# Softmax times V for 96 heads: products of two heads packed densely into one accumulator, with zeros beside each head's probabilities

## The chip, the core and the metric

The kernel runs on one NeuronCore of a Trainium2 chip. The metric is the time of one execution on the device in microseconds (us); lower is better. A core has a matrix engine (PE, whose weight loads are listed as PEld), a vector engine (DVE), an activation engine (ACT), a general engine (POOL) and a queue engine (SP) that here only issues DMA transfers. The engines run side by side, each takes its own instructions in order, and they wait for each other by semaphores: counters that an instruction raises when it has finished and that another engine's instruction waits on.

## What is computed

```python
batch, n_heads, seq, head_dim = 8, 12, 1024, 64
scores: [8, 12, 1024, 1024] float32      v: [8, 12, 1024, 64] float32

attn = np.exp(scores - scores_max)
attn = attn / (np.sum(attn, axis=-1, keepdims=True) + 1e-8)
return np.matmul(attn, v)
```

There are 96 heads. The scores are 402.7 MB, V and the output 25.2 MB each. The fast path leaves the maximum out (exp of the raw score), takes the row sums from a column of ones beside V, and checks at the end that all sums and all V lay in a safe range ("the verdict"); if they did not, a slow general path computes everything anew. With the inputs used here the general path is not taken.

## The kernel before, in words

**Tiling.** Two heads form a pair (T = 2). A pair's scores are loaded as one tile s_nat of 128 partitions: partitions 0 to 63 belong to the first head, 64 to 127 to the second, and each partition holds R = 16 whole score rows of 1024 keys (8.4 MB). So "row r" below means 128 score rows, 64 of each head. The loop `For_i` (L423) has 24 iterations; each handles four heads, that is K = 2 pairs, k = 0 and k = 1. There is one s_nat buffer for each k.

**One row** (function heads, L366 on):
- ACT computes exp of two rows at once into p_nat (L377; eight buffers of two rows). In the second half of k = 1 it takes one row at a time ("late" rows).
- PE turns the row: eight transposes of 128x128 into psT (L390), each a weight load and a matmul. After it, psT holds for each chunk c of 128 keys: keys on the partitions, 128 columns, 64 for each head.
- DVE copies two rows (one if late) from psT to pt in SBUF (L402, late L398). psT and pt have two buffers of two rows each.
- PE multiplies (function finish, L152): for each of the eight chunks, pt's 128 columns are the weights and `vones` of both heads the moving data: 64 columns of V of head 0, two columns of ones, 64 columns of V of head 1, together M = 130. All eight accumulate into 130 columns of psO. Head 0's rows against head 1's V, and the reverse, are computed too and never read.
- A row is multiplied LAG = 3 rows after it was turned. After each G = 3 rows, DVE takes the reciprocals of the sums (L132) and multiplies: once for partitions 0 to 63 and once for 64 to 127, since the useful columns differ (L140). This is function normalise; with 16 rows there are six groups for each k.

**Around it.** POOL spreads the loaded V into `vones` as half-precision (spread_v, L248). In the middle of k = 0 DVE takes the largest absolute value of `vones` (watch_v, L259, with two small operations at L269). At the end of every iteration DVE and PE work out the verdict so far (judge: two reductions at L285 and L286, small operations at L289 and L292, a product of one column at L297 on PE, a copy at L301).

**Order of the transfers.** SP issues them in one order written out by hand: in an iteration the next pair for k = 0 (load_first, after the last exp of k = 0), the store of k = 0, then in function last the next pair for k = 1, the store of k = 1 and the next V. A load waits until exp has read the buffer. For the very last pairs the loads are cut into parts: two halves for k = 0 of the last iteration, and 4, 4, 3, 2, 1, 1, 1 rows for k = 1 of the last iteration. The nested `If` arms of last choose between these. The stores of the last pair are issued by end (L185).

**What sets the order on PE.** The helper in_line chains every transpose and product in program order, so PE does: turn row r, multiply row r - 3, turn row r + 1, and so on. Every weight load and every matmul of the built program raises PE's one semaphore by one, and all other engines wait on its value. That holds for the changed program as well: it has 769 weight loads and 769 matmuls in an iteration's body, the old one 513 and 513.

Of the kernel before, what the change touches and what calls it, by code (L numbers as in the profile page):

```python
# [9 lines left out]
FP16 = mybir.dt.float16  # L10
# [16 lines left out]
def kernel(  # L27
# [25 lines left out]
    T = 2  # L53
# [28 lines left out]
    s_bufs = buffers(sb_pool, K, [P, R, SK], FP32, "s_nat")  # L82
    v_sb = sb_pool.tile([P, C // L, S, L, D], FP32, name="v_sb")
    p_bufs = buffers(sb_pool, 8, [P, EB, SK], FP16, "p_nat")
    pt_bufs = buffers(sb_pool, 2, [P, EB, SK], FP16, "pt")
    out_bufs = buffers(sb_pool, K, [P, R, D], FP32, "out_sb")
    small_pool = ctx.enter_context(tc.tile_pool(name="small", bufs=1))
    seen = small_pool.tile([P, 1 + K * R + 1], FP32, name="seen")
# [34 lines left out]
            after(dma, queued[-1])  # L123
        queued.append(dma)

    def invert(k, st, g):

        rows = min(G, R - g * G)
        psO = st["psO"][g][:, 0 : rows * M].rearrange("p (g m) -> p g m", m=M)
        at = 1 + k * R + g * G  # L130
        recip = seen[:, at : at + rows].rearrange("p (g o) -> p g o", o=1)
        nc.vector.reciprocal(out=recip, in_=psO[:, :, D : D + 1])  # L132
        return psO, recip

    def normalise(k, st, g):
        psO, recip = invert(k, st, g)
        rows = min(G, R - g * G)
        for t in range(T):
            part = slice(t * W, (t + 1) * W)
            nc.vector.tensor_tensor(  # L140
                out=out_bufs[k][part, g * G : g * G + rows, :],
                in0=psO[part, :, t * N : t * N + D],
                in1=recip[part].to_broadcast([W, rows, D]),
                op=ALU.mult,
            )

    def finish(u):

        n0, k, r, pt, st = u
        g, i = r // G, r % G  # L150
        for c in range(C):
            product = nc.tensor.matmul(  # L152
                out=st["psO"][g][:, i * M : (i + 1) * M],
                lhsT=pt[:, c * P : (c + 1) * P],
                rhs=vones[:, k, c].rearrange("p t n -> p (t n)")[:, 0:M],
                start=(c == 0),
                stop=(c == C - 1),
            )
            in_line(product)
        if i == G - 1 or r == R - 1:  # L160
            normalise(k, st, g)
        if r == R - 1 and k < K - 1:
            spread_v(k)
            store(n0, k)
# [14 lines left out]

    def end():  # L180

        cut = (GROUPS - 2) * G
# [10 lines left out]
    watches = []  # L193
# [50 lines left out]
    def spread_v(k):  # L244

        for t in range(T):
            for s in range(S):
                spread = nc.gpsimd.tensor_copy(  # L248
                    out=vones[s * Q : (s + 1) * Q, k, :, t, 0:D].rearrange(
                        "i (h l) d -> i h l d", l=L  # L250
                    ),
                    in_=v_sb[(k * T + t) * Q : (k * T + t + 1) * Q, :, s],
                )
                for watch in watches:
                    apart(spread, watch, "products in between")

    def watch_v(behind):

        watch = nc.vector.tensor_reduce(  # L259
            out=most,  # L260
            in_=vones[:, :, :, :, 0:D].rearrange("p k c t d -> p k (c t) d"),
            axis=mybir.AxisListType.XYZ,
            op=ALU.max,
            apply_absolute_value=True,
        )
        after(watch, behind)
        watches.append(watch)
        for bound, op in ((V_MIN, ALU.is_ge), (V_MAX, ALU.is_le)):
            nc.vector.scalar_tensor_tensor(  # L269
                out=fits, in0=most, scalar=bound, in1=fits, op0=op, op1=ALU.mult  # L270
            )
# [6 lines left out]
    most, fits, right = small("most"), small("fits"), small("right", FP16)  # L278
    nc.gpsimd.memset(fits, 1.0)

    def judge(bank):

        n = K * R
        part = small("part")
        nc.vector.tensor_reduce(out=seen[:, 0:1], in_=seen[:, 0 : n + 1], axis=X, op=ALU.min)  # L285
        nc.vector.tensor_reduce(  # L286
            out=seen[:, n + 1 : n + 2], in_=seen[:, 1 : n + 2], axis=X, op=ALU.max
        )
        nc.vector.scalar_tensor_tensor(  # L289
            out=part, in0=seen[:, n + 1 : n + 2], scalar=1.0, in1=fits, op0=ALU.is_le, op1=ALU.mult  # L290
        )
        nc.vector.scalar_tensor_tensor(  # L292
            out=right, in0=seen[:, 0:1], scalar=1.0 / SUM_MAX, in1=part, op0=ALU.is_ge, op1=ALU.mult
        )
        cell = bank[0:1, G * M : G * M + 1]
        in_line(
            nc.tensor.matmul(  # L297
                out=cell, lhsT=right[:], rhs=vones[:, 0, 0, 0, D : D + 1], start=True, stop=True
            )
        )  # L300
        nc.vector.tensor_copy(out=count[:], in_=cell)  # L301

    def general():
# [8 lines left out]
        nc.gpsimd.memset(s_bufs[0][:, 3, 0 : C * (D + 1)], 1.0)  # L312
        half = SK // 2
        with tc.For_i(0, BH * C, 1, iteration_sync="reg_based") as n:
            nc.sync.dma_start(out=row, in_=s_rows[bass.ds(n, 1)].rearrange("o p j -> (o p) j"))
            nc.sync.dma_start(
                out=v1[:, :, 0:D], in_=v_rows[bass.ds(n // C, 1)].rearrange("o p c d -> (o p) c d")
            )
# [24 lines left out]
            nc.sync.dma_start(  # L343
                out=o_rows[bass.ds(n, 1)].rearrange("o p d -> (o p) d"), in_=out_row
            )

    def last(n0):

        before = queued[-1:]
        k = K - 1  # L350
        with tc.If(n0 < BH - AHEAD) as cmp:
            spread_v(k)
            with tc.If(n0 < BH - 2 * AHEAD) as cmp2:
                queued[:] = before
                load(k, (n0 + (AHEAD + T * k)) % BH)
                store(n0, k)
                load_v((n0 + 2 * AHEAD) % BH)
            with cmp2.Else():
                queued[:] = before
                load(k, BH - T, (4, 4, 3))  # L360
                store(n0, k)
                load(k, BH - T, (2, 1, 1, 1), 11)
        with cmp.Else():
            queued[:] = before
            end()

    def heads(n0):

        for k in range(K):
            st = dict(psO=[take(psO_bufs) for g in range(GROUPS)])  # L370
            for r in range(R):
# [23 lines left out]
                    in_line(turned)  # L395
                    other_bank(psT2, r % EB, turned)
                if late:
                    copy = nc.vector.tensor_copy(out=pt, in_=psT)  # L398
                    rewrite(pt2, copy)
                    other_bank(psT2, r % EB, copy)  # L400
                elif r % EB == EB - 1:
                    copy = nc.vector.tensor_copy(out=pt2[:], in_=psT2[:])  # L402
# [12 lines left out]

    assert BH % AHEAD == 0 and BH >= 2 * AHEAD and SK == Q * S * C and K == 2
    load_v(0)
    for k in range(K):
        load(k, T * k, (R // 2, R // 2) if k == 0 else (R,))
    for k in range(K):  # L420
        spread_v(k)
    load_v(AHEAD)
    with tc.For_i(  # L423
        0, BH, AHEAD, iteration_sync="reg_based"
# [41 lines left out]
```

## Time and profile before

| quantity | value |
|---|---|
| time, median of three runs | 1070.16 us (1069.1 to 1070.58) |
| the profiled execution's own time | 1069.46 us |
| its span, first to last instruction | 1067.5 us |
| mean granted PE clock | 0.897 of full |
| bytes moved by DMA | 453.06 MB, mean 424 GB/s, queue busy 98.6% of the span |
| PE busy, with 12312 matmuls | 793.6 us |
| DVE busy | 768.8 us |
| ACT busy | 737.3 us |
| exp of two rows (L377) | 1899 ns each |
| copy of two rows (L402) | 1224 ns each |
| normalise, 64x192 (L140) | 355 ns each, two for a group |
| watch_v's reduction (L259) | 2286 ns each, one in an iteration |

The span is what the profile covers; the execution's time is 1.96 us longer. Busy times are sums over the span; matmuls overlap each other, so PE's busy time is not a measure of how close it is to its limit. The distance between the starts of successive matmuls is: in a row of eight transposes at full clock the trace has starts 55 to 56 ns apart, in products of 130 columns 56 and 59 in turn.

### The profile page before, as it was taken

To read this page: it belongs to the slowest core of one execution; us is meant where nothing else is said; L and a number is where in the kernel's file an instruction comes from. 1 tells how busy PE (TensorE), PEld (TensorE's weight loads), DVE (VectorE), ACT (ScalarE), POOL (GpSimd) and SP (SyncE) were. 2 spreads that over 40 slices of the span, in tenths; PEclk is the share of its full clock that TensorE was granted. 3 is DMA by queue.
4 is the path that set the end of the run, shared out by engine and by line. 5 is a ranking of instruction groups with operands and counts; after the bars stand their busy time and mean duration, and the time that the engine had idled before them with its cause. 6 is when DMAs were issued, how large, how long until landed. Compare 5 with 4: busy or idle time off the path is not lost.

```text
span 1067.5 us, 32791 instructions
## 1 busy us (share of the span) xinstructions
PE 793.6 (74%) x12312; PEld 757.7 (71%) x12312; DVE 768.8 (72%) x1539; ACT 737.3 (69%) x504; POOL 239.2 (22%) x399
## 2 busy tenths in 40 slices
PE   2578768786786777867878668776786777866887
PEld 2578668686686776867768668776686777866877
DVE  1578767696686866867769667785686866867788
ACT  3567568666686576856867668667686586756893
POOL 3031131211311203113121131221311303113121
PEclk9889889898898988989989889898898988989899
DMA  9999999999999999999999999999999999999993
GB/s 393 441 438 413 422 462 413 452 413 431 453 413 452 426 419 449 417 433 446 440 425 449 425 423 452 413 428 456 413 452 413 431 453 413 452 410 434 432 429 151
DMA packets 18580, 453.06 MB, mean 424 GB/s; under 512 B 2064, under 2 KB 2192, under 8 KB 8720
## 3 DMA queue, kind: packets, MB, share of 16 engines
q1 hardware_dynamic: 18576, 452.99, 98.6%
q8 instruction: 4, 0.07, 0.0%
HBM read 637.53 MB, written 25.17 MB: 621 GB/s over the span
## 4 chain that ended last, share of the span: by engine, by line
DMA 58%; ACT 27%; issue 6%; PE 3%; PEld 2%; DVE 2%; ACTq 1%; SPq 0%; PEldq 0%; DVEq 0%
DMA s_nat<-in_scores_dram 58%; ACT p_nat L377 26%; PE psO L152 1%; PEld L390 1%; PE psT L390 1%; DVE pt L402 1%; PEld L152 1%; ACTq L377 1%; DVE most L259 0%; ACT L377 0%; DVE pt L398 0%; SPq L219 0%; ACTq L423 0%; DVE seen L132 0%; DVE out_sb L140 0%
## 5 line engine op out<-in xcount | busy, mean ns | idle before, releaser
L377 ACT ACTIVATE p_nat<-s_nat 128x2048 f16<-128x2048 f32 (+1 forms) x480 | 706.5, 1557 | 118.9 <-PE psO L152 42.5
L390 PE MATMUL psT<-ident,p_nat 128*128 128x128 f16 x6144 | 505.4, 232 | 166.2 <-ACT p_nat L377 166.2
L390 PEld LDWEIGHTS <-p_nat 128*128 128x128 f16 x6144 | 425.1, 118 | 176.0 <-ACT p_nat L377 176.0
L402 DVE COPY pt<-psT 128x2048 f16<-128x2048 f16 x288 | 352.4, 1224 | 261.5 <-PE L390 165.2
L152 PE MATMUL psO<-vones,pt 128*128 128x130 f16 x6144 | 486.6, 223 | 62.9 <-DVE fits L269 40.4
L152 PEld LDWEIGHTS <-pt 128*128 128x128 f16 x6144 | 387.8, 99 | 84.7 <-DVE pt L402 55.6
L248 POOL CAST vones<-v_sb 32x512 f16<-32x512 f32 x392 | 238.5, 608 | 813.4 <-PE psT L390 318.6
L140 DVE TENSOR_TENSOR out_sb<-psO,seen 64x192 f32<-64x192 f32 (+1 forms) x576 | 191.8, 333 | 18.0
L377 ACT ACT_TABLE_LOAD x24 | 30.8, 1283 | 195.4 <-DMA s_nat<-in_scores_dram 178.5
L398 DVE COPY pt<-psT 128x1024 f16<-128x1024 f16 x192 | 123.5, 685 | 2.3
L259 DVE TENSOR_REDUCE most<-vones 128x1 f32<-128x2048 f16 x24 | 54.9, 2286 | 0.7
L132 DVE RECIPROCAL seen<-psO 128x3 f32<-128x3 f32 (+1 forms) x288 | 49.3, 171 | 2.8 <-PE L390 1.4
L297 PE MATMUL psO<-vones,right 128*1 128x1 f16 x24 | 3.9, 164 | 41.0 <-DVE right L292 41.0
L297 PEld LDWEIGHTS <-right 128*1 128x1 f16 x24 | 1.9, 79 | 45.3 <-DVE right L292 45.3
L301 DVE CAST count<-psO 1x1 int32<-1x1 f32 x24 | 3.5, 146 | 6.2 <-PE psO L297 6.2
L269 DVE SCALAR_TENSOR_TENSOR fits<-most,fits 128x1 f32<-128x1 f32 x48 | 7.4, 155 | 0.0
L289 DVE SCALAR_TENSOR_TENSOR part<-seen,fits 128x1 f32<-128x1 f32 x24 | 5.3, 220 | 0.8
L285 DVE TENSOR_REDUCE seen<-seen 128x1 f32<-128x33 f32 x24 | 4.5, 188 | 0.8
L292 DVE SCALAR_TENSOR_TENSOR right<-seen,part 128x1 f16<-128x1 f32 x24 | 3.9, 162 | 0.8
L286 DVE TENSOR_REDUCE seen<-seen 128x1 f32<-128x33 f32 x24 | 4.2, 177 | 0.0
L77 DVE MEMSET vones<- 128x64 f16 x1 | 0.1, 112 | 0.8 <-PEq L450 0.8
L74 DVE CAST ident<-ident 128x128 f16<-128x128 f32 x1 | 0.2, 227 | 0.4 <-POOL ident masks.py:199 0.4
(8 smaller groups left out, 1.1 us busy)
## 6 DMA issues: line engine op xcount, KB each, us to landing
s_nat<-in_scores_dram SPq DMA_DIRECT2D x50, 4096.0 KB, 18.7
v_sb<-in_v_dram SPq DMA_DIRECT2D x24, 1024.0 KB, 22.2
out_dram<-out_sb SPq DMA_DIRECT2D x47, 512.0 KB, 16.8
s_nat<-in_scores_dram SPq DMA_DIRECT2D x2, 2048.0 KB, 22.8
s_nat<-in_scores_dram SPq DMA_DIRECT2D x1, 1536.0 KB, 27.5
s_nat<-in_scores_dram SPq DMA_DIRECT2D x3, 512.0 KB, 20.8
s_nat<-in_scores_dram SPq DMA_DIRECT2D x1, 1024.0 KB
s_nat<-in_scores_dram SPq DMA_DIRECT2D x47, 28.4
```

The source lines that it names most:

```text
L132: nc.vector.reciprocal(out=recip, in_=psO[:, :, D : D + 1])
L140: nc.vector.tensor_tensor(out=out_bufs[k][part, g * G : g * G + rows, :], in0=psO[part, :, t * N : t * N + D], in1=recip[part].to_broadcas ...
L152: product = nc.tensor.matmul(out=st["psO"][g][:, i * M : (i + 1) * M], lhsT=pt[:, c * P : (c + 1) * P], rhs=vones[:, k, c].rearrange("p t ...
L248: spread = nc.gpsimd.tensor_copy(out=vones[s * Q : (s + 1) * Q, k, :, t, 0:D].rearrange("i (h l) d -> i h l d", l=L), in_=v_sb[(k * T + t) ...
L259: watch = nc.vector.tensor_reduce(out=most, in_=vones[:, :, :, :, 0:D].rearrange("p k c t d -> p k (c t) d"), axis=mybir.AxisListType.XYZ, ...
L269: nc.vector.scalar_tensor_tensor(out=fits, in0=most, scalar=bound, in1=fits, op0=op, op1=ALU.mult)
L289: nc.vector.scalar_tensor_tensor(out=part, in0=seen[:, n + 1 : n + 2], scalar=1.0, in1=fits, op0=ALU.is_le, op1=ALU.mult)
L297: nc.tensor.matmul(out=cell, lhsT=right[:], rhs=vones[:, 0, 0, 0, D : D + 1], start=True, stop=True)
L377: exp = nc.scalar.activation(out=p_nat[:, g : g + rows, :].rearrange("p r (x v) -> p x r v", v=Q * L), in_=s_bufs[k][:, r + g : r + g + ro ...
L390: turned = nc.tensor.transpose(out=psT[:, c * P : (c + 1) * P], in_=p_row[:, c // L, c % L, :], identity=ident16[:],)
L398: copy = nc.vector.tensor_copy(out=pt, in_=psT)
L402: copy = nc.vector.tensor_copy(out=pt2[:], in_=psT2[:])
```

## The change

1. **Products.** `pt` gets a second copy slot for each chunk: shape [128, 2 rows, C = 8, T = 2, T = 2, W = 64]. For each chunk there are now two blocks of 128 columns. Block 0 holds head 0's 64 columns and 64 zeros, block 1 holds 64 zeros and head 1's columns. The zeros are set once, ahead of the loop; the copies write only slots 0 and 3 of the four (apart_columns). finish issues two products for each chunk, one for each block, each with the 65 columns of its own head (M = 65: V and one column of ones). All sixteen accumulate into the same 65 columns of psO, so partitions 0 to 63 get head 0 and 64 to 127 head 1.
2. **Normalise.** G is 4 and the output of both heads lies in the same columns: one reciprocal and one multiplication over 128 partitions for four rows; four groups for each k.
3. **Watch and verdict.** watch_v reads v_sb (the loaded V in single precision) and no longer `vones`. It stands once ahead of the loop and then in function last, at the end of an iteration, behind the second spread_v, in the arm that all but the last iteration take. The two reductions of judge become fold and stay at the end of every iteration; the rest of judge moves to the arm of the last iteration only, behind the last stores.
4. **Transfers.** In the third iteration from the end, the next pair for k = 1 is loaded in two halves (a third nested `If`). The general path issues its transfers from ACT's queue.
5. **Last rows.** For the last two rows of k = 1 the lag is 2 and no longer 3.

```diff
-    G = 3
+    G = 4
-    M = T * N - 2
-    GROUPS = -(-R // G)
+    M = D + 1
+    GROUPS = R // G
-    pt_bufs = buffers(sb_pool, 2, [P, EB, SK], FP16, "pt")
+    pt_bufs = buffers(sb_pool, 2, [P, EB, C, T, T, W], FP16, "pt")
+    for buf in pt_bufs:
+        nc.vector.memset(buf[:], 0.0)
...
-        for t in range(T):
-            part = slice(t * W, (t + 1) * W)
-            nc.vector.tensor_tensor(
-                out=out_bufs[k][part, g * G : g * G + rows, :],
-                in0=psO[part, :, t * N : t * N + D],
-                in1=recip[part].to_broadcast([W, rows, D]),
-                op=ALU.mult,
-            )
+        nc.vector.tensor_tensor(
+            out=out_bufs[k][:, g * G : (g + 1) * G, :],
+            in0=psO[:, :, 0:D],
+            in1=recip.to_broadcast([P, G, D]),
+            op=ALU.mult,
+        )
+    def apart_columns(at):
+        return at[:, :, 0 : 2 * T : 2 * T - 1, :]
...
         for c in range(C):
-            product = nc.tensor.matmul(
-                out=st["psO"][g][:, i * M : (i + 1) * M],
-                lhsT=pt[:, c * P : (c + 1) * P],
-                rhs=vones[:, k, c].rearrange("p t n -> p (t n)")[:, 0:M],
-                start=(c == 0),
-                stop=(c == C - 1),
-            )
-            in_line(product)
+            for t in range(T):
+                product = nc.tensor.matmul(
+                    out=st["psO"][g][:, i * M : (i + 1) * M],
+                    lhsT=pt[:, c, t].rearrange("p u j -> p (u j)"),
+                    rhs=vones[:, k, c, t, 0:M],
+                    start=(c == 0 and t == 0),
+                    stop=(c == C - 1 and t == T - 1),
+                )
+                in_line(product)
...
-    def watch_v(behind):
-        watch = nc.vector.tensor_reduce(
+    def watch_v():
+        nc.vector.tensor_reduce(
             out=most,
-            in_=vones[:, :, :, :, 0:D].rearrange("p k c t d -> p k (c t) d"),
-            axis=mybir.AxisListType.XYZ,
+            in_=v_sb[:].rearrange("p h s l d -> p (h s l d)"),
+            axis=X,
             op=ALU.max,
             apply_absolute_value=True,
         )
-        after(watch, behind)
...
-    def last(n0):
+    def last(n0, bank):
         with tc.If(n0 < BH - AHEAD) as cmp:
             spread_v(k)
+            watch_v()
             with tc.If(n0 < BH - 2 * AHEAD) as cmp2:
-                queued[:] = before
-                load(k, (n0 + (AHEAD + T * k)) % BH)
-                store(n0, k)
-                load_v((n0 + 2 * AHEAD) % BH)
+                with tc.If(n0 < BH - 3 * AHEAD) as cmp3:
+                    queued[:] = before
+                    load(k, (n0 + (AHEAD + T * k)) % BH)
+                    store(n0, k)
+                    load_v((n0 + 2 * AHEAD) % BH)
+                with cmp3.Else():
+                    queued[:] = before
+                    load(k, BH - 2 * AHEAD + T * k, (R // 2, R // 2))
+                    store(BH - 3 * AHEAD, k)
+                    load_v(BH - AHEAD)
...
         with cmp.Else():
             queued[:] = before
             end()
+            judge(bank)
...
-                    copy = nc.vector.tensor_copy(out=pt2[:], in_=psT2[:])
+                    copy = nc.vector.tensor_copy(
+                        out=apart_columns(pt2[:].rearrange("p r c t u j -> p (r c) (t u) j")),
+                        in_=psT2[:].rearrange("p r (c t j) -> p (r c) t j", t=T, j=W),
+                    )
...
-                if k == 0 and r == R // 2 - 1:
-                    watch_v(copy)
...
-                if len(pending) > LAG:
+                while len(pending) > (LAG - 1 if late and r >= R - EB else LAG):
                     finish(pending.pop(0))
         while pending:
             finish(pending.pop(0))
-        last(n0)
-        judge(st["psO"][-1])
+        fold()
+        last(n0, st["psO"][-1])
```

More of the change, by code (lines that the diff above doesn't have):

```diff
@@ L124, in queue, with normalise @@
         queued.append(dma)
-    def invert(k, st, g):
-        rows = min(G, R - g * G)
-        psO = st["psO"][g][:, 0 : rows * M].rearrange("p (g m) -> p g m", m=M)
+    def normalise(k, st, g):
+        psO = st["psO"][g][:, 0 : G * M].rearrange("p (g m) -> p g m", m=M)
         at = 1 + k * R + g * G
-        recip = seen[:, at : at + rows].rearrange("p (g o) -> p g o", o=1)
+        recip = seen[:, at : at + G].rearrange("p (g o) -> p g o", o=1)
         nc.vector.reciprocal(out=recip, in_=psO[:, :, D : D + 1])
[L133 to L137, printed above, removed]
-        for t in range(T):
-            part = slice(t * W, (t + 1) * W)
-            nc.vector.tensor_tensor(
-                out=out_bufs[k][part, g * G : g * G + rows, :],
-                in0=psO[part, :, t * N : t * N + D],
-                in1=recip[part].to_broadcast([W, rows, D]),
-                op=ALU.mult,
-            )
+        nc.vector.tensor_tensor(
[6 more added lines that the diff above has]
+        return at[:, :, 0 : 2 * T : 2 * T - 1, :]
     def finish(u):
@@ L180, in end @@
     def end():
-        cut = (GROUPS - 2) * G
+        cut = (GROUPS - 1) * G
         for a, b in ((0, cut), (cut, R)):
@@ L265, in watch_v @@
         )
-        after(watch, behind)
-        watches.append(watch)
         for bound, op in ((V_MIN, ALU.is_ge), (V_MAX, ALU.is_le)):
@@ L279, with fold @@
     nc.gpsimd.memset(fits, 1.0)
-    def judge(bank):
+    def fold():
         n = K * R
-        part = small("part")
         nc.vector.tensor_reduce(out=seen[:, 0:1], in_=seen[:, 0 : n + 1], axis=X, op=ALU.min)
@@ L288, in judge @@
         )
+    def judge(bank):
+        n = K * R
+        part = small("part")
         nc.vector.scalar_tensor_tensor(
@@ L314, in general @@
         with tc.For_i(0, BH * C, 1, iteration_sync="reg_based") as n:
-            nc.sync.dma_start(out=row, in_=s_rows[bass.ds(n, 1)].rearrange("o p j -> (o p) j"))
-            nc.sync.dma_start(
+            nc.scalar.dma_start(out=row, in_=s_rows[bass.ds(n, 1)].rearrange("o p j -> (o p) j"))
+            nc.scalar.dma_start(
                 out=v1[:, :, 0:D], in_=v_rows[bass.ds(n // C, 1)].rearrange("o p c d -> (o p) c d")
@@ L397, in heads @@
                 if late:
-                    copy = nc.vector.tensor_copy(out=pt, in_=psT)
+                    copy = nc.vector.tensor_copy(
+                        out=apart_columns(pt.rearrange("p c t u j -> p c (t u) j")),
+                        in_=psT.rearrange("p (c t j) -> p c t j", t=T, j=W),
+                    )
                     rewrite(pt2, copy)
@@ L412, in heads @@
             finish(pending.pop(0))
-        last(n0)
-        judge(st["psO"][-1])
-    assert BH % AHEAD == 0 and BH >= 2 * AHEAD and SK == Q * S * C and K == 2
+        fold()
+        last(n0, st["psO"][-1])
+    assert BH % AHEAD == 0 and BH >= 3 * AHEAD and SK == Q * S * C and K == 2
     load_v(0)
@@ L421 @@
         spread_v(k)
+    watch_v()
     load_v(AHEAD)
```

13 lines of the change are left out of this document (6 added, 7 removed).

## Prediction, on record before the changed kernel had run

> **What bounds the kernel now.** I read the page's engine shares, its slices and its groups first, then the chain, then the timeline of one iteration and of the last 70 us.
>
> ```profile
> PE 793.6 (74%) x12312; PEld 757.7 (71%) x12312; DVE 768.8 (72%) x1539; ACT 737.3 (69%) x504; POOL 239.2 (22%) x399
> ...
> PEclk9889889898898988989989889898898988989899
> DMA  9999999999999999999999999999999999999993
> ...
> DMA 58%; ACT 27%; issue 6%; PE 3%; PEld 2%; DVE 2%; ACTq 1%; SPq 0%; PEldq 0%; DVEq 0%
> ...
> L152 PE MATMUL psO<-vones,pt 128*128 128x130 f16 x6144 | 486.6, 223 | 62.9 <-DVE fits L269 40.4
> ```
>
> No engine is near full, the DMA row is full until the last slice, and the chain is transfers and the exps that free their buffers. Over 24 iterations that is 43.6 us each (in the chain the same exps start at 463.38 and 506.96). PE is not on the path, but not far off: within a burst its eights of transposes and of products start 0.45 us apart without a gap, 0.91 us a row, 29.1 us for an iteration's 32 rows.
>
> The second thing to see is when DVE may start behind PE. From the timeline of one burst:
>
> ```profile
> 484.95 1.04 PE L390 MATMUL psT<-ident,p_nat 128*128 128x128 f16 x8
> 486.04 1.23 DVE L402 COPY pt<-psT 128x2048 f16<-128x2048 f16 x1 [2.56 <-PE L152]
> 488.38 0.61 PE L390 MATMUL psT<-ident,p_nat 128*128 128x128 f16 x8
> 489.06 1.23 DVE L402 COPY pt<-psT 128x2048 f16<-128x2048 f16 x1 [0.31 <-PE psO L152]
> 490.20 0.61 PE L390 MATMUL psT<-ident,p_nat 128*128 128x128 f16 x8
> 490.98 1.22 DVE L402 COPY pt<-psT 128x2048 f16<-128x2048 f16 x1 [0.19 <-PE psO L152]
> ```
>
> Each copy waits for the eight transposes above it, and DVE was idle each time (brackets). Yet it starts 0.05, 0.07 and 0.17 us after they end: the longer PE has run at full clock, the later the signal. The trace also keeps the time of each semaphore increment, and these three copies start 22 to 24 ns behind the last increment they need. Of PE's 24,629 increments, 23,208 stand exactly 30 ns behind the one before and none closer. At half clock a pair (weight load and matmul) takes 107 ns, and its two increments stand 30 and 77 ns apart; at full clock a pair takes 56 to 57 ns but its two increments 60, so they fall behind, by 20 increments at the end of that burst. **PE's signals have a rate of one per 30 ns**, and today's pairs just exceed it without harm.
>
> **The change, part by part.**
>
> *Products.* A row has 8 transposes and 8 products now, 16 pairs; afterwards 8 and 16, 24 pairs. PE's own pace for a product of 65 columns is in no row. Above, it is bounded by the 57 ns of 130 columns; below, by half of that, 28 ns, as the columns are half. Weight loads do not raise the lower end: at a burst's start two follow each other by 15 ns. Within these bounds the pace does not matter if each increment takes 30 ns: 48 increments make 1.44 us a row, against 0.93 to 1.36 us of PE's work. 32 rows make 1536 increments, **46.1 us an iteration, more than the 43.6 us of the transfers**. PE's signals become the bound, and ACT, DVE and the loads, which all wait for them, are paced by it. Copies are no bound: 2.88 us pass per two rows, of which DVE needs 1.22 and a share of the normalise.
>
> *Copies.* They write runs of 64 elements with gaps. No row shows such a copy. Lower end 1224 ns, the same elements in one run (L402); upper end one element at a time, by the slope of L140's forms (355 ns for 192 elements, 222 for 64: 1.04 ns each): 2048 x 1.04 + 0.15 = 2.28 us. I take 1.22, as the nearest row has the same types and sources, and keep 2.28 for the range.
>
> *Normalise.* 24 of 64x192 or 64x64 become 8 of 128x256 an iteration; by the same slope 355 + 64 x 1.04 = 0.42 us. DVE saves 191.8 - 192 x 0.42 = 111 us, and 16 for the reciprocals, all off the path, so I count it as nothing except at the ends of iterations.
>
> *Watch at the iteration's end.* Its 2.29 us stood in the middle of k = 0 and cost PE 1.7 us (40.4 us in 24 waits on L269). Now it stands, on DVE's queue, between the last normalise and the next iteration's first copy, and PE can turn only four rows before it needs that copy. From the last increment of an iteration: reciprocal and multiplication 0.6, fold 0.3 (L285 to L286), watch 2.29, its two small operations 0.4, branches 0.9 (DVE's branch instructions at the boundary at 1026.4 run to 1027.3): the copy starts at 4.5, ends at 5.7, and the first product signals at 5.9 us. The four turned rows' 64 increments are done by about 3 us and hidden; the other 1472 take 44.2. Sum: **50.1 us**. The wait of some 3 us lets the clock drop: after the 2 us wait ahead of 484 the page's timeline has 0.83 to 1.04 us for eight transposes and not 0.45, for 3.4 us; two such rows add 0.4 each, bounds 0 and 0.8, I take 0.4: **50.5 us**. The transfers (43.6) and POOL's spreading (5.3 us) fit beside it.
>
> *Judge in the last arm.* It takes away a 1.7 us wait of PE (L297, 41.0 us in 24) at each boundary, and puts PE's wait for its own signals in its place, counted above. *Halves and shorter lag* only move transfers and rows that no longer bound: nothing. *Memsets ahead of the loop*, twice 2048 words, some 2.3 us each by 1.04 ns: DVE has no copy before 22.08, hidden.
>
> *Sum.* The first iteration waits for its second pair as before: that pair's first transpose starts at 47.69. From there 16 rows of transposes and 19 of products signal, 256 + 608 = 864 increments, 25.9 us: 73.6. Then 23 x 50.5 = 1161.5: 1235.1. From the last product to the end as now (1061.27 + 0.64 to 1067.5) 5.6: span 1240.7. With the 1.96 us between span and time: **1243 us**, +173 on the profiled 1069.46; the median of the runs is 0.7 us above that, which is nothing here.
>
> [...]
>
> **The rivals.**
>
> *1. Faster: the signals are no limit.* If increments only look paced (they might be coalesced or recorded so), PE does 0.93 us a row and 29.8 an iteration, the transfers stay the bound, and the tail shortens. Today the tail is PE's, as the last rows of ACT's timeline and of the chain show:
>
> ```profile
> 1046.76 4.86 ACT L377 ACTIVATE p_nat<-s_nat 128x1024 f16<-128x1024 f32 x5 [0.85 <-PE L390]
> ```
>
> ```profile
> 1059.14 1.39 PE psO L152 x24
> ```
>
> Exp is done at 1051.6, PE's products only at 1061.9. The halves let the exps of the next-to-last iteration's k = 1 start behind those of k = 0, 4.7 us earlier (ACT waits from 1000.4 to 1005.1); the judge's 1.7 and the watch's 1.7 us go. Together 8.1, up to 11 with the lag: 1058 to 1062, I say **1060**. For it: the tail gains are real, and one burst's lag of 0.6 us is the most that the trace shows. Against it: copies do wait for the increments. [...] Chance 0.27. This is the case on the other side. It decides from 25 ns per increment down, where 5.9 + 1472 x 0.0256 = 43.6 us brings an iteration back under the transfers.
>
> *2. The 30 ns hold, but the boundary is hidden* (the watch runs beside PE's backlog): 46.1 + 1 us of branches, 73.6 + 23 x 47.1 + 7.5 = **1164 us**. The queue order on DVE speaks against it. With partial costs, and with somewhat quicker increments, 1100 to 1220. Chance 0.13.
>
> *3. No limit by signals, but pairs of 43 to 46 ns*, weight load and matmul one after the other (15 + 28 to 31): the 64 rows of the tail lose 16 x 13 to 16 ns each, 13 to 16 us, all that rival 1 gains: **1068 to 1080 us**. Against it, the weight load is wholly hidden in today's 56 ns pairs. Chance 0.05.
>
> *4. Slow copies on top*: 1.06 us more at each boundary, 24 us: **1267 us**. Chance 0.05.
>
> **How the numbers follow.** My forecast, 1243 with 1215 to 1262, has 0.50; then 0.27, 0.13, 0.05, 0.05. Cases of both signs are in play, so 8 in 10 must reach down to rival 1, of which some lies below 1059: 1059 to 1260 leaves out about 0.1 on either side. Differences under 0.2% (2 us) are what a measurement here cannot tell from none. Faster by more: rival 1, 0.27. Within: a part of rival 3, 0.03. Slower: the rest, 0.70.
>
> **What the profile would show.** Right: an iteration of 50 us in the chain, with PE, its semaphore and DVE on it and not the transfers; increments 30 ns apart nearly throughout; eights of products bunched at 30 to 57 ns and then waiting; DMA busy about 85%; DVE idle most of the time on PE; the watch between two iterations with PE waiting for pt right after it. Products of 65 columns below 60 ns a pair throughout a long burst, with copies that follow at once, would make it wrong, and so would a DMA row still full of nines.

## The result, and the profile after

| | before | changed |
|---|---|---|
| time, median | 1069.21 us (1069.1 to 1070.58) | 1258.76 us (1258.24 to 1259.79, 5 runs) |
| profiled execution, span | 1069.46, 1067.5 us | 1259.42, 1257.7 us |
| one iteration, mean of 23 | 43.6 us | 51.2 us |
| mean granted PE clock | 0.897 | 0.930 |

The change makes the kernel slower, by a factor of 1.177 (95% interval 1.1754 to 1.1786). The forecast was 1243 us. From the page of the changed kernel, the engines, the DMA slices, the chain and the two groups on it (busy us, mean ns of one, idle before):

```profile
PE 1073.2 (85%) x18433; PEld 1032.0 (82%) x18433; DVE 657.8 (52%) x992; ACT 766.4 (61%) x504; POOL 239.3 (19%) x399
...
DMA  9999999898898799988989989989898798988930
...
PE 60%; DVE 30%; issue 4%; DMA 3%; PEld 1%; DVEq 1%; ACT 0%; SPq 0%; PEldq 0%
...
L152 PE MATMUL psO<-vones,pt 128*128 128x65 f16 x12288 | 721.8, 195 | 93.1 <-DVE pt L412 72.9
...
L412 DVE COPY pt<-psT 128x2048 f16<-128x2048 f16 x288 | 349.2, 1219 | 263.8 <-PE psO L152 197.7
```

The transfers were 58% of the chain before and are 3% now; PE and the copies that wait for it have taken their place, and the DMA row is no longer full (87% of the span, mean 360 GB/s). The copies with gaps cost what the dense ones did, 1219 ns to 1224. The mean of 195 ns for a product says nothing of its pace, since products overlap: 61% of the starts of all matmuls are 59 to 61 ns behind the one before. The chain of the changed kernel over one iteration (start us, us, what):

```profile
629.21 0.93 PE psO L152 x16
630.14 0.51 PE psT L397 x8
630.65 0.93 PE psO L152 x16
...
639.88 2.20 DVE most L256
644.02 1.23 DVE pt L412
645.39 0.76 PE psO L152 x16
...
690.62 2.20 DVE most L256
694.76 1.24 DVE pt L412
696.13 1.11 PE psO L152 x16
697.24 0.85 PE psT L397 x8
```

Two things are to be seen. First, a row lasts 1.44 us (629.21 to 630.65), with no wait of PE in it: 24 pairs at 60 ns each, weight load and product of 65 columns as well as weight load and transpose. That is 48 increments of 30 ns. Second, the watch (639.88) comes between two iterations, and the first copy stands right behind it at 644.02.

In the trace, 35,894 of the 36,894 increments of PE's semaphore are exactly 30 ns behind the one before, and none closer than 29. PE itself is not so slow. This is the timeline just behind a boundary, that is, between two iterations, where PE has waited and no increments are outstanding (an increment is outstanding when its instruction has started and it has not gone out yet):

```profile
644.02 2.35 DVE L412 COPY pt<-psT 128x2048 f16<-128x2048 f16 x2 [1.43 <-PE psT L397]
...
646.44 0.67 PE L152 MATMUL psO<-vones,pt 128*128 128x65 f16 x16
646.92 0.48 PEld L397 LDWEIGHTS <-p_nat 128*128 128x128 f16 x8
...
647.40 0.67 PE L152 MATMUL psO<-vones,pt 128*128 128x65 f16 x16
```

Here a row takes 0.96 us (646.44 to 647.40), and its products start 29 to 36 ns apart. In the next row, among the sixteen products that begin at 648.36, the distance of the starts goes from 29 to 36 ns to 60, and so it goes again after each later wait for a copy. So here PE runs ahead of its signals for a while and is then held at their rate, 60 ns for two. The count of outstanding increments says when: at each boundary it starts from none and rises to 63, in every iteration, and never above; in the kernel before it never passes 29. These fast rows also settle a rival: their weight loads raise the semaphore like all others and their products still start 29 to 36 ns apart, so here it is not the signal of a weight load as such that keeps it from running beside a product. Over the whole run 22% of the starts are under 40 ns behind the one before.

### The profile page after: what moved, and what is told of

Same layout as the page of the kernel before. It is cut to its first block, busy times and chain, and to the rows that moved or that the text cites. A ratio compares the mean times of both kernels' runs of the same rounds, so it can differ in the third digit from the quotient of the medians.

```text
span 1257.7 us, 44669 instructions
## 1 busy us (share of the span) xinstructions
PE 1073.2 (85%) x18433; PEld 1032.0 (82%) x18433; DVE 657.8 (52%) x992; ACT 766.4 (61%) x504; POOL 239.3 (19%) x399
## 4 chain that ended last, share of the span: by engine, by line
PE 60%; DVE 30%; issue 4%; DMA 3%; PEld 1%; DVEq 1%; ACT 0%; SPq 0%; PEldq 0%
PE psO L152 42%; DVE pt L412 22%; PE psT L397 18%; DVE most L256 4%; DMA s_nat<-in_scores_dram 3%; DVE pt L405 1%; PEld L152 1%; DVE fits L264 1%; PEld L397 1%; DVE seen L134 0%; DVE seen L279 0%; DVEq L354 0%; DVEq L435 0%; DVE out_sb L135 0%; DVE seen L280 0%
## 5 line engine op out<-in xcount | busy, mean ns | idle before, releaser
L384 ACT ACTIVATE p_nat<-s_nat 128x2048 f16<-128x2048 f32 (+1 forms) x480 | 735.6, 1565 | 317.6 <-PE psO L152 179.2
L152 PE MATMUL psO<-vones,pt 128*128 128x65 f16 x12288 | 721.8, 195 | 93.1 <-DVE pt L412 72.9
L152 PEld LDWEIGHTS <-pt 128*128 128x128 f16 x12288 | 648.9, 99 | 131.7 <-DVE pt L412 52.8
L397 PE MATMUL psT<-ident,p_nat 128*128 128x128 f16 x6144 | 521.0, 234 | 84.7 <-DVE seen L280 54.9
L397 PEld LDWEIGHTS <-p_nat 128*128 128x128 f16 x6144 | 435.9, 118 | 87.2 <-issue 57.0
L412 DVE COPY pt<-psT 128x2048 f16<-128x2048 f16 x288 | 349.2, 1219 | 263.8 <-PE psO L152 197.7
L405 DVE COPY pt<-psT 128x1024 f16<-128x1024 f16 x192 | 132.5, 690 | 107.2 <-PE psO L152 106.5
L134 DVE RECIPROCAL seen<-psO 128x4 f32<-128x4 f32 x192 | 35.3, 184 | 210.0 <-PE L397 131.4
L135 DVE TENSOR_TENSOR out_sb<-psO,seen 128x256 f32<-128x256 f32 x192 | 81.5, 425 | 11.3 <-DVE seen L134 5.4
L256 DVE TENSOR_REDUCE most<-v_sb 128x1 f32<-128x2048 f32 x24 | 54.6, 2276 | 0.3 <-DMA v_sb<-in_v_dram 0.3
L296 PE MATMUL psO<-vones,right 128*1 128x1 f16 x1 | 0.2, 165 | 2.8 <-DVE right L291 2.8
```

What stands on the lines that cost most here:

```text
L135: nc.vector.tensor_tensor(out=out_bufs[k][:, g * G : (g + 1) * G, :], in0=psO[:, :, 0:D], in1=recip.to_broadcast([P, G, D]), op=ALU.mult,)
L152: product = nc.tensor.matmul(out=st["psO"][g][:, i * M : (i + 1) * M], lhsT=pt[:, c, t].rearrange("p u j -> p (u j)"), rhs=vones[:, k, c, ...
L256: nc.vector.tensor_reduce(out=most, in_=v_sb[:].rearrange("p h s l d -> p (h s l d)"), axis=X, op=ALU.max, apply_absolute_value=True,)
L384: exp = nc.scalar.activation(out=p_nat[:, g : g + rows, :].rearrange("p r (x v) -> p x r v", v=Q * L), in_=s_bufs[k][:, r + g : r + g + ro ...
L397: turned = nc.tensor.transpose(out=psT[:, c * P : (c + 1) * P], in_=p_row[:, c // L, c % L, :], identity=ident16[:],)
L405: copy = nc.vector.tensor_copy(out=apart_columns(pt.rearrange("p c t u j -> p c (t u) j")), in_=psT.rearrange("p (c t j) -> p c t j", t=T, ...
```

## The experiments

Theory 1 is the forecast's: PE's increments go out at one per 30 ns, 48 a row, and set the pace. The other theories say that PE's own work does: by the moving columns (theory 2) or by the weights (theory 3). Ratios are to the kernel before.

**e1: half the columns.** Products of 33 columns: the second half of V and the ones; the result is written twice, so the first half of each output row holds the second half's values.

```diff
-    M = D + 1
+    M = D // 2 + 1
...
-                    rhs=vones[:, k, c, t, 0:M],
+                    rhs=vones[:, k, c, t, D + 1 - M : D + 1],
```

> The changed kernel with products of 33 moving columns in place of 65: it multiplies only the second half of V's columns and the column of ones, and writes that half twice. Weight loads, matmuls and their increments stay as many. Theory 1 (one increment per 30 ns sets PE's pace): no change, 1258 us within 5. Theory 2 (the columns that are streamed set it): each product is 13 ns shorter, 512 in an iteration, 6.8 us less in each of 24, some 1100 us.

Measured: 1248.58 us, 1.167 (1.165 to 1.1689), against 1258.76 for the changed kernel. Half the columns are worth 0.8%, 10.2 us. That is twice the 5 us that theory 1 allowed, but far from the 1100 us of theory 2, which falls. The 10 us are in the iterations: all take 50.7 to 50.9 us here, where the changed kernel has 50.7 and 51.7 in turn. While the granted clock is at half (0.50 from 697 to 700 us in the changed kernel), products of 65 columns start 53 to 57 ns apart in the changed kernel and products of 33 columns 28 ns apart here, so that here a row at half clock, 8 x 107 + 16 x 28 ns or 1.30 us, stays under the increments' 1.44. 36,017 of 36,894 increments stand 30 ns apart.

**e2: half the weights.** Each head's 64 columns of pt are the weights, onto 64 partitions; the zeros are not read. What is computed stays the same.

```diff
-                    out=st["psO"][g][:, i * M : (i + 1) * M],
-                    lhsT=pt[:, c, t].rearrange("p u j -> p (u j)"),
+                    out=st["psO"][g][t * W : (t + 1) * W, i * M : (i + 1) * M],
+                    lhsT=pt[:, c, t, t],
...
```

> The changed kernel with products that load only a head's own 64 columns as weights and write 64 partitions of the accumulator, so that the zeros are not read. As many instructions and increments, half the weight columns. Theory 1: no change, 1258 us within 5. Theory 3 (the weight loads with their zero columns set the pace, 128 columns for 64 useful ones): clearly faster, below 1200 us.

Measured: 1257.26 us, 1.1755 (1.1736 to 1.1775), which is the changed kernel's time within a measurement's error. Theory 3 falls: with half the weights and the same number of instructions nothing changes.

**e3 and e4: the kernel before, with tiny pairs added.** A pair is a weight load and its matmul. Eight (e3) or four (e4) products of one column with one column of weights behind each row; nobody reads them. Everything else stays as before the change.

```diff
             in_line(product)
+        for x in range(8):
+            extra = nc.tensor.matmul(
+                out=st["psO"][g][0:1, 400:401],
+                lhsT=vones[:, 0, 0, 0, D : D + 1],
+                rhs=vones[:, 0, 0, 0, D : D + 1],
+                start=True, stop=True,
+            )
+            in_line(extra)
```

> The kernel before, with eight more pairs behind each row's products, each one weight load and one matmul of a single column into an unused column. It adds the number of increments that the change adds and hardly any column work. Theory 1: 48 increments a row, 46.1 us an iteration, and some 3 us at its boundary (verdict, branches, first copy): 73.6 + 23 x 49 + 7.6 = 1208 us, 1150 to 1220. Theories 2 and 3: at most 28 ns for each extra pair, 1.13 us a row, 36 us an iteration, under the transfers' 43.6; only the tail grows, 32 x 0.22 = 7 us: 1076 us.

> The same with four more pairs. Theory 1: 40 increments a row, 1.2 us, 38.4 us an iteration and 3 at its boundary, still under 43.6: the transfers bound again and the tail's 32 rows take 0.29 us more each, 1079 us. Theories 2 and 3: 32 x 0.11 = 3.6 us more, 1073 us. If the increments had no fixed rate but each pair cost the same, it would lie halfway between the kernel before and the run with eight.

Measured: e3 1259.86 us, 1.1776 (1.1757 to 1.1796), and e4 1098.04 us, 1.026 (1.0243 to 1.0277). Eight pairs that multiply next to nothing cost the same 190 us as the whole change (the kernel before took 1070.33 us beside these runs). The page of e3 shows the same exchange on the chain and in the DMA row:

```profile
DMA  9999889988898899989998889879998998988930
...
PE 73%; DVE 13%; issue 5%; PEld 4%; DMA 3%; ACT 1%; DVEq 0%; SPq 0%; PEldq 0%; ACTq 0%
```

They are not free for PE itself, though. Early in an iteration, with 26 to 46 increments outstanding, a row of e3 takes 1.30 us by its own pace (0.91 before; the bound expected was 1.13): the first tiny product starts 150 ns behind the product before it, the others 25 ns apart, and the first two transposes behind them 96 and 84 ns apart. Late in the iteration, with 58 to 61 outstanding, it takes 1.44 us. So 32 x 1.30 = 41.6 us and the boundary's 4.9 would have passed the transfers' 43.6 in any case, by 2.9 us of the 7.5 that an iteration of e3 grew, an estimate; the signals added the rest. From e3's chain, starts of a row's transposes early and late:

```profile
652.57 0.57 PE psT L399 x8
...
653.87 0.57 PE psT L399 x8
...
682.04 0.57 PE psT L399 x8
...
683.48 0.57 PE psT L399 x8
```

And e4's timeline has rows 1.20 us apart:

```profile
641.23 0.62 PE L152 MATMUL psO<-vones,pt 128*128 128x130 f16 x8
...
642.43 0.62 PE L152 MATMUL psO<-vones,pt 128*128 128x130 f16 x8
...
643.63 0.62 PE L152 MATMUL psO<-vones,pt 128*128 128x130 f16 x8
```

That is as long as 40 increments of 30 ns, but here PE is not held by them: never more than 11 are outstanding, and its own starts add up to the same 1.20 us (e3's 1.30 less four tiny products of 25 ns). So e4 does not tell the signals from PE's own work.

The first four pairs cost 27.7 us, the next four 161.8. Here a limit is crossed, and there is no price per pair: with four, the rows make 32 x 1.2 = 38.4 us an iteration, below the transfers' 43.6, and only the boundary brings it to 44.4 (2.2 us of waiting for judge, 1.0 for branches, the rest mostly rows at half clock). Both numbers of theory 1 were missed, by 52 and 19 us, mostly for one reason, the boundary: e3's was expected at 3 us and took about 5 (1.96 us of PE waiting for judge, 1.03 for branches, 1.9 in rows at half clock: 46.1 + 4.9 = 51.0 of the 51.15 measured), and e4's, expected to hide under the transfers, took 6.

**e5: the watch back in the middle.** The changed kernel with watch_v behind a copy in the middle of k = 0.

```diff
             spread_v(k)
-            watch_v()
...
+                if k == 0 and r == R // 2 - 1:
+                    watch_v(copy)
...
```

> The changed kernel with the watch moved back to the middle of k = 0 (it still reads the loaded V). Theory of the boundary: the watch on DVE's queue holds up the next iteration's first copy; without it PE's increments pause about 1.5 us at a boundary (branches 1.06, the first copy 0.45) and not 4.6 to 5.6, 23 times 3.1 to 4.1 us less: 1165 to 1190 us, if 1.2 us of backlog and the slack of a copy hide the watch in the middle. Rival (the pause is PE's own, from its wait for its signals and its branches): within 10 us of 1258.

Measured: 1211.62 us, 1.1325 (1.1307 to 1.1342), 47 us below the changed kernel. The iterations fall from 51.19 to 48.72 us, 23 x 2.47 = 57 us. PE's wait for the first copy is gone: the only pause over 0.5 us in an iteration's increments is that of the branches, 1.03 to 1.09 us. Ten of the 57 us are lost again in the first iteration, which ends 10 us later, since the watch now waits there for the second V on DVE's queue (start us, us, idle before):

```profile
48.12 2.29 DVE L256 TENSOR_REDUCE most<-v_sb 128x1 f32<-128x2048 f32 x1 [17.30 <-DMA v_sb<-in_v_dram]
```

So the place of the watch cost the iterations 57 of the change's 190 us, and moving it back gained 47, less than the 69 to 94 expected. The rest is the rate: 46.1 + 1.0 us of branches + some 1.4 us of rows at half clock (741 increments in the run stand 60 to 130 ns apart, some 46 ns too long each) make 48.5 of the 48.7.

**e6, e7, e8: the rest of the change without the dense products.** e6 is the changed kernel with the products, copies and normalise of before. e7 is the kernel before with nothing but the pair in two halves. e8 is e6 without the halves. The cut shows the halves:

```diff
...
+                with tc.If(n0 < BH - 3 * AHEAD) as cmp3:
...
+                with cmp3.Else():
+                    queued[:] = before
+                    load(k, BH - 2 * AHEAD + T * k, (R // 2, R // 2))
+                    store(BH - 3 * AHEAD, k)
+                    load_v(BH - AHEAD)
...
```

> All the rest of the change with the products, the copies and the normalise of before: watch at the iteration's end, verdict in the last arm, halves, lag 2 for the last rows. Theory (only the products cost, and the tail gains are real): 1058 to 1062 us, 8 to 11 less than before. Rival (the transfers end at 1047 whatever PE does and the end moves little): 1066 to 1070.

> The kernel before with one edit: the next pair for k = 1 in the third iteration from the end comes in two halves. Theory: the exps of k = 1 start 4.7 us earlier there, and PE's chain to the end with them, less what PE's own queue of rows takes back: 1064 to 1067 us. Rival (PE is the bound of the tail already ahead of that point): 1069, no change.

> As the run of the rest, without the halves: watch at the end, verdict in the last arm, lag 2. Theory: the judge's wait of 1.7 us between the last two iterations and the watch's 1.7 us in the last one go: 1064 to 1067 us. Rival (ACT's exps set the tail, and PE only follows): 1069.

| | time, us | ratio (interval) | last eight products start, us, in the profiled execution |
|---|---|---|---|
| before, beside these runs | 1069.53 (1069.2 to 1071.05) | | 1061.27 |
| e7, halves alone | 1067.93 (1067.13 to 1068.38) | 0.9981 (0.9972 to 0.999) | 1060.32 |
| e8, all but the halves | 1070.4 (1068.49 to 1071.45) | 1.0009 (1.0 to 1.0018) | 1060.60 |
| e6, both | 1063.92 (1063.33 to 1065.63) | 0.9949 (0.9935 to 0.9962) | 1057.68 |

e6 beats both kernels, by 5.6 us or 0.5% against before; it is the version to keep. The halves alone are worth 1.6 us, hardly more than a measurement tells here, the other edits alone nothing, both together 5.6. All three lie above what was expected, e6 by 2 us, e7 by 1 and e8 by 3. Where it is gained is seen on the timeline of e6, whose exps end almost when they do before (1051.40 and 1051.62 us):

```profile
1046.54 4.86 ACT L385 ACTIVATE p_nat<-s_nat 128x1024 f16<-128x1024 f32 x5 [0.80 <-PE psO L153]
```

```profile
1057.68 0.63 PE L153 MATMUL psO<-vones,pt 128*128 128x130 f16 x8 [0.74 <-DVE pt L406]
```

What is gained is PE's backlog behind the exps: 1061.27 - 1051.6 = 9.7 us of it before, 1057.68 - 1051.4 = 6.3 us in e6. (The profiled execution of e6 was its slowest, 1065.63 us, so this shows 3.4 us and not the whole gain.) The halves give PE its rows earlier, but before the change PE then still stands at the watch and at judge, and without the halves the time saved at those is spent waiting for exp. This fits the table but was not tested; no run separates lag, watch and judge.

**e9: increments by themselves.** A kernel that computes nothing of the task, PE alone, run once:

```diff
...
+            pairs(2, 65)
+            pairs(3, 65, signal=True)
+            pairs(4, 65, extra=True)
+            pairs(5, 65, signal=True, extra=True)
+            pairs(6, 33)
+            pairs(7, 33, signal=True)
...
```

> This kernel leaves the whole task out: no scores are read, and it writes one 128x64 tile. PE does seven stages of 256 products, each stage with a wait at its end: (1) 130 columns and (2) 65 columns, each without a semaphore increment but for the last; (3) 65 columns, an increment on every product; (4) a further weight load ahead of every product, no increments; (5) the same with an increment on the weight load and on the product; (6) 33 columns without and (7) with an increment on every product. Theory 1, the increments themselves go out at one per 30 ns: stage 5 runs at 60 ns a pair, 15.4 us, as in the changed kernel, while stage 4, the same instructions without increments, is quicker by more than 10%, 28 to 53 ns a pair; stage 3 is no slower than stage 2 by more than what lifts it to 30 ns, and stage 7 at 30 ns however quick stage 6 is. The rival, that what is limited is the handling or recording of finished instructions, whether they signal or not: stages 4 and 5 take the same time, within 3%, and so do 2 and 3, 6 and 7; the 60 ns a pair would then be there without any semaphore.

In this program a product's own weight load raises nothing. From the stretches of the trace that lie within stages 2, 4, 5 (late), 6 and 7 (late): window, us, PE busy (instructions), PEld busy, clock, DMA share, GB/s. The count takes in products that reach over the edges, each about 0.2 us long, so the pace is (length + 0.2) / count:

```profile
18.00:24.00 6.00, 6.00 (x204) 6.00 (x201) 1.00 0.01 3
...
36.00:48.00 12.00, 12.00 (x211) 12.00 (x209) 1.00 0.01 3
...
60.00:64.00 4.00, 4.00 (x65) 4.00 (x64) 1.00 0.01 4
70.00:72.50 2.50, 2.50 (x107) 2.50 (x104) 1.00 0.00 0
77.00:80.00 3.00, 3.00 (x96) 3.00 (x93) 1.00 0.00 0
```

By the starts: a pair of 65 columns without increments takes 30.4 ns (stage 2), of 33 columns 25.0 ns (stage 6). With an increment on each product, 33 columns run at 25.0 ns until 31 increments are outstanding, with one pause of 0.47 us on the way, and from about the 145th at 34.2 ns (stage 7). With a second weight load, 57.8 ns without increments (stage 4); with two increments 57.8 ns for the first 170 pairs or so, then 64.2 ns (stage 5). Stage 3 keeps up 30.4 ns for some 220 products, while its increments go out 34 ns apart and fall behind by 1 us; then it too has 31 outstanding, and the rest start 34 ns apart.

The rival falls: the same instructions are quicker without increments (25.0 against 34.2 ns, 30.4 against 34). The numbers outstanding, 31 and 42 here and 63 in the changed kernel, would be one bound, an estimate, if all of PE's instructions are counted, those without an increment too: 31 pairs of two are 62 instructions, 21 pairs of three (two increments each) 63. Theory 1 stands, with two corrections. Stages 4 and 5 were expected to differ by over 10% and differ by 3.5% on the mean, 11% once PE is held; the second weight load of a pair costs 27 ns itself here (57.8 - 30.4), so this pair of stages separates little. And the rate here was 34 ns for products and 30 for weight loads, where the whole kernels have 30 for both; what makes the 4 ns is open.

**e10: the kernels' rows by themselves.** PE alone again, run once, in rows of eight transposes with eight products of 130 columns (kinds 2 and 3) or sixteen of 65 (kinds 4 and 5).

> This kernel leaves the whole task out: no scores are read, and one 128x64 tile is written. PE does rows in the form of the two kernels, 32 of each kind, with a wait behind each kind: (1, 2) eight transposes and eight products of 130 columns with no increments, twice (the first to warm up), (3) the same with an increment on every matmul; (4) eight transposes and sixteen products of 65 columns with no increments, (5) the same with an increment on every matmul. Weight loads raise nothing here. After the run before this, in which a pair of 65 columns took 30 ns without increments and increments of products went out 34 ns apart, theory 1 expects: kind 2 0.91 us a row, as in the kernel before; kind 4 8 x 56 + 16 x 30 = 0.93 us a row; kind 5, with 24 increments instead of the 48 of the changed kernel, 24 x 34 = 0.82 us a row, which is below 0.93, so no or little more than kind 4, 0.93 to 0.96. So PE's own pace would leave the changed row where the old one was, and the 1.44 us were its signals alone. A rival in which PE itself is slow with two weight loads for a chunk gives 1.2 us a row or more in kind 4.

The timeline of e10, in kind 2 and then in kind 4:

```profile
60.47 0.62 PE L59 MATMUL psO<-vones,pt 128*128 128x130 f16 x8
...
61.42 0.62 PE L59 MATMUL psO<-vones,pt 128*128 128x130 f16 x8
...
111.16 0.65 PE L59 MATMUL psO<-vones,pt 128*128 128x65 f16 x16
...
112.18 0.65 PE L59 MATMUL psO<-vones,pt 128*128 128x65 f16 x16
```

The old row takes 0.951 us and the changed one 1.012, on the mean of 32, with or without an increment on each matmul. (Expected were 0.91 and 0.93; transposes took 62 ns here.) So the change costs PE 0.06 us a row in work, 32 x 1.012 = 32.4 us an iteration, far below the transfers' 43.6. The other 0.43 of the changed kernel's 1.44 us is put down to its signals; e10's increments, half as many, leave the row at 1.012 us. The changed kernel with fewer increments was not tried: in it every weight load and matmul raises the semaphore, which the kernel's text does not decide.

## Why the prediction was right, point by point

The forecast's mechanism and size held: +190 us where +173 was forecast, inside the forecast's own range of 1215 to 1262. By its steps:

- **What bounds the kernel now, and the signals' rate.** Right. 30 ns to the nanosecond, and e3 shows rows of 1.44 us in the old kernel too, where PE's own pace would have been 1.30. What had not been said is that PE is held by its signals as well: in the changed kernel not only do readers learn late, the instructions themselves fall to 60 ns a pair once 63 increments are outstanding.
- **Products, 1.44 us a row, 46.1 us an iteration.** Right to the digit. The bounds on PE's own pace (28 to 57 ns, said not to matter) hold too: 30.4 ns in e9, and 1.012 us a row in e10, within the 0.93 to 1.36 (8 x 57 + 16 x 28 ns would have made the lower end 0.90). The 30 ns for a product of 65 columns that 0.93 takes (8 x 56 + 16 x 30), and rival 3's 28 to 31, were the forecast's estimates; no run had shown them, and e9 shows 30.4.
- **Copies and normalise.** 1219 and 690 ns for copies against 1.22 assumed; the upper bound of 2.28 and rival 4 are out. Normalise 425 ns, forecast 0.42. The memsets took 1.77 us each (2.3 estimated) and were hidden.
- **Watch at the iteration's end.** Right in kind, 0.5 us short. From the last product's increment (639.03) to the copy's start (644.02) it took 5.0 us and not 4.5, to the first product's increment (645.47) 6.4 and not 5.9. Term by term: reciprocal and multiplication 0.6, fold 0.2, watch 2.3, small operations 0.5, and 1.4 for the branches where 0.9 were counted, from 642.59 to 644.02. At the next boundary they take the same; DVEq is DVE's sequencer:

```profile
693.17 0.12 DVE fits L264
...
693.33 0.09 DVEq L354
...
694.67 0.04 DVEq L473
...
694.76 1.24 DVE pt L412
```

  **The mis-sized term is DVE's branches**, read from one boundary of the old kernel; the one more nested `If` of last may be the reason, which no run separates.
- **Half clock, 0.4 us.** It took 0.6: the mean iteration is 51.19 us, less 6.44 and 44.16. The size of this term is in part luck. The forecast had two rows at half clock behind every boundary; instead boundaries alternate. At one, the rows behind the wait run at full clock, as shown above (1.00 from 645.4 to 650 us); at the next, three rows do not (0.53 from 696 to 702), as the chain behind 694.76 shows with 1.11 and 0.85 us for sixteen products and eight transposes. Hence the iterations of 50.7 and 51.7 us, and hence what e1 gained: at half clock a row of the changed kernel takes 0.85 + 0.88 = 1.73 us, more than its increments' 1.44.
- **The sum.** First iteration 74.95 us (73.6 forecast), 23 x 51.19 = 1177.4 (1161.5), the end 5.4 (5.6): 1257.7. Of the 17.0 us missed, 15.9 are the two terms of the boundary, 1.4 the first iteration.
- **Rival 1, no limit by signals (0.27).** Wrong in its main part and right in its side: e10 shows that PE by itself does a row in 1.012 us, and e6, which has what it counted for the tail, gives 1063.92, nearly its 1060. Of the 8.1 us that it put on the tail, 5.6 were there.
- **Rival 2, boundary hidden (0.13).** Out: PE waits 1.5 to 2.7 us for the first copy at each boundary. With the watch elsewhere (e5) it comes nearest, 1211.62, and still not to 1164, since 1.4 us an iteration at half clock and 10 us in the first iteration remain. Of the quicker increments in its range there is no sign: in neither kernel do two stand closer than 29 ns.
- **Rival 3, pairs of 43 to 46 ns (0.05).** Out: 30.4 ns by themselves, 60 with their signals.
- **Rival 4, slow copies (0.05).** Out, as said above.
- **A misreading without effect.** The chain's rows at 463.38 and 506.96 are stretches of issue (the engine waits for nothing that the profile shows); the exps behind them start at 464.64 and 508.21. The 43.6 us between them are the same.

## What to carry to other kernels

Count the semaphore increments of the matrix engine, weight loads included: in these two kernels none went out closer than 29 ns behind the one before and most at 30, and long stretches of pairs that each raise the semaphore twice ran at 60 ns a pair, with products of 65 columns (the changed kernel) as with products of one (e3). So here each product of 130 columns, a pair of 57 ns, became two pairs of 60 ns. Look in the trace for increments at one constant distance; here the start of a burst did not show it in its own pace (three rows in the changed kernel, 145 to 220 pairs in e9). And a part of a change can be worth keeping without its headline: e6 gained 5.6 us, though neither of its two parts gained more than 1.6 alone.

## What the runs showed of the hardware that was not expected

- PE ran ahead of its own increments by no more than a certain number: 63 outstanding in the changed kernel, in e9 42 with two increments a pair and 31 with one. Counted in PE's instructions, with those that raise nothing, that is 62 or 63 each time. Once there, its pairs started at the rate of the increments (64.2 and 34.2 ns in e9, 60 in the changed kernel).
- A product of one column with one column of weights, which raises the semaphore twice with its load, took as long as one of 65 columns that does, once PE was held: the tiny products at e3's iteration ends start 60 ns apart, like those of the changed kernel.
- The granted clock after the same wait was not the same each time: in the changed kernel three rows run at half clock behind one boundary (0.85 us for eight transposes at 697.24) and none behind the one before (a row of 0.96 us at 646.44). The granted clock is 0.53 from 696 to 702 us and 1.00 from 645.4 to 650, and iterations of 50.7 and 51.7 us follow each other in turn, with one exception.
- Going from products with 128 columns of weights to products with one and back cost PE time of its own in e3: 150 ns from the last of the one to the first of the other, then 25 ns each, and 96 and 84 ns for the first two transposes behind them; e4's rows of 1.20 us are e3's 1.30 less four of the 25. What makes it is open.
- The copy that writes runs of 64 elements, with a gap of 128 behind every second one, took what the dense one takes, 1219 ns to 1224.
